# Output weights of a hybrid decoder layer: float16 halves and block sums prepared beside the attention and kept in DRAM, and all token tiles by block products

## The chip, the cores and the metric

The kernel runs on one core of a Trainium2 chip. The metric is the device time of one execution in microseconds (us), as the median of several runs. Beside it stands one profiled execution, from which every duration below is read. The engines are PE (TensorE, matrix products; PEld is its weight load), DVE (VectorE), ACT (ScalarE), POOL (GpSimd) and SP (SyncE, which here issues the DMAs). Each engine runs its own list of instructions in a fixed order.

## The reference

One layer over 2048 tokens (and 16 learned meta tokens ahead of them) of width 1024. Three mixers read one normalised input through one projection, and one output projection joins them:

```python
hn = rms_norm(h, pre_g)
proj = hn @ w_in                       # q, k, v, forget gate, GLA and RG-LRU columns
y_fox = fox_attention(q, k, v, log_f) * silu(fg)      # 8 heads of 64: width 512
y_gla = gla_chunked(...)  * silu(gg)                  # width 512
y_lru = rg_lru(...)       * silu(lg)                  # width 1024
y = concatenate([y_fox, y_gla, y_lru])                # 2048 wide
h = h + rms_norm(y @ w_out, post_g)                   # w_out is 2048 x 1024
```

`fox_attention` is causal softmax attention with a term c[t] - c[s] in the logit, c being the running sum of the log forget gates. Everything is float32; the kernel forms a float32 product from float16 halves, a value x scaled and split into hi + lo, and three products hi·hi, hi·lo and lo·hi.

## The kernel before, in words

The program is a list of jobs. Each job has a main part and a part that prepares the next job; `merge` (L155) takes them in turn, so that the matrix products of one fill the waits of the other. After that a scheduler puts the instructions of each engine in a fixed order. First come the projections and the mixing of GLA and of the LRU, up to about 890 us; then FoX, from 891 to 1706 us; then the output projection.

**FoX** goes over 4 pairs of heads p and 4 chunks c of 512 queries, 16 jobs, called (p,c) here. `fox_attend` (L1236 on) takes blocks of 128 keys one after another: 8 products into the one score pair `sq` (L1257), an Exp on ACT (`pt`, L1265), row sums on DVE and POOL (`za`, L1273), and 4 products with the values (`fv`, L1281). It ends with the row sums (`fx`, L1292), which go to DRAM and back in small steps (L499, L501, L506, L1299), a product on POOL (L1300) and the store of y (L1301).

Beside it `fox_prepare` of the next job projects keys, queries and values (L476, L488) and the gate, takes the maximum of every query block's scores (`mj` on DVE, L1207), and sends the maxima to the rows of `qx` by six small DMAs (`dr`, L1230). The first products of the next attend with `KX` wait for these. The gate (`fox_gate`) stands in the generator `rest`, whose pieces are handed out between the maxima. The weights of head pair p+1 are loaded by `load_dma` (L412) in jobs (p,1) and (p,3), and made into halves by ACT and DVE (L433, L434).

**The output projection** in its two forms. Tiles of 128 tokens 0 and 1 are done in 4 quarters of 256 columns and tiles 2 and 3 in 2 halves of 512 columns, by plain products over 16 k-tiles times 3 (`out_part`, L1566). The other 12 tiles are done as 6 pairs: y of a pair (256 x 2048) is cut into blocks A11, A12, A21, A22, and w_out into B11 to B22; with the sums S1 to S4 of the A and T1 to T4 of the B (T1 = B12 - B11, T2 = B22 - T1, T3 = B22 - B12, T4 = B21 - T2) seven block products of 24 matmuls give all four results (`out_pair`, L1586):

```python
def product(nm, w):            # 8 k-tiles, three float16 products each
    for kt in range(KT):
        for j, (a, b) in enumerate(((yh, wh), (yh, wl), (yl, wh))):
            nc.tensor.matmul(out=ps, lhsT=a[:, kt, :], rhs=b(kt), ...)
```

For this w_out is read from DRAM twice. `wout_begin` and `wout_end` take it in four column groups q (16 loads of 512 KB, a Square with a sum on ACT for the scale, then halves by ACT L1359 and DVE L1360); this begins in job (1,2) and goes on through (3,2), (3,3) and the first tiles. `sums_begin` and `sums_end` load it again (16 loads), form the T on POOL (L1386, L1390) and DVE (L1388, L1392) and split them into `ts`; they are placed among the plain tiles by a table in `project_out`. The y of a tile comes back from DRAM, is squared for its scale (L1418), and its maximum sum goes through one small product (`mx`, L463) before the halves are made.

The lines that the change and the prediction name are L412 to L415 (load of weights), L1188 (where `rest` holds the gate), L1230 to L1232 (dr), L1301 (store of y), and L1308 to L1480 with the table in `project_out`.

Of the kernel before, what the change touches and what calls it, by code (L numbers as in the profile page):

```python
# [21 lines left out]
P = 128  # L22
# [55 lines left out]
PLAIN = 4  # L78
OB = 27
# [8 lines left out]
class Ctx:  # L88
# [9 lines left out]
        "T": 3, "ZZ": 4, "WC": 1, "OO": 3, "OX": 2, "LV": 5, "AT": 2, "AC": 2, "GV": 6, "GG": 6, "GS": 6, "M": 1, "MV": 1, "YG": 2, "RS": 2, "ZS": 1, "ZA": 2, "PT": 6, "ED": 2, "KT": 1, "Z": 1, "WH": 1, "WL": 1, "XC": 4, "X": 16, "L0": 4, "L1": 4, "L2": 2, "L3": 2, "L4": 6}  # L98
# [68 lines left out]
def hybrid_kernel(tc, xT, x, w_grp, w_fa, vecs, w_a2, w_r, w_i, w_out, post_g, masks, out, yD=None):  # L167
    nc = tc.nc
    with ExitStack() as es:
# [13 lines left out]
        k.laD = k.dram.tile([P, T], F32, name="laD")  # L183
        k.xp = es.enter_context(tc.tile_pool(name="xhat", bufs=1))
# [4 lines left out]
        k.sent, k.begun, k.todo, k.wbegun, k.ybegun = [], [], [], [], []  # L189
# [19 lines left out]
        for t in range(8):  # L209
            for c in range(len(LP)):  # L210
# [20 lines left out]
        drain(jobs[0][1])
        for i, (_, _, mix, n_main, _) in enumerate(jobs):
# [8 lines left out]
            if i >= len(jobs) - 2:  # L241
# [326 lines left out]
def lru_mix(k, t, c, flush):  # L568
# [32 lines left out]
    for t, c, a, v, xc, h, gate in jobs:  # L601
# [9 lines left out]
        nc.sync.dma_start(out=k.yD[1024 + P * t:1024 + P * t + P, a0 - NM:u0 + n - NM], in_=y[:, a0 - u0:n])  # L611
# [555 lines left out]
def fox_prepare(k, p, c):  # L1167
# [20 lines left out]
    rest = chain(*([fox_values(k, p, 0)] if c == 0 else []), fox_values(k, p, c + 1), fox_gate(k, p, c))  # L1188
# [39 lines left out]
    for h in range(2):  # L1228
        for t in range(3):
            nc.sync.dma_start(out=qx[64 * h + t:64 * h + t + 1, :].rearrange("o (i q) -> o i q", q=P),  # L1230
                              in_=dr[4 * h:4 * h + 4, t, :])
    yield from rest  # L1232
    st["q", p, c] = qh, ql, qx


def fox_attend(k, p, c):  # L1236
# [64 lines left out]
    k.store = nc.sync.dma_start(out=k.yD[P * p:P * p + P, CH * c:CH * c + CH], in_=o).ins  # L1301

def out_begin(k):

    nc = k.nc  # L1308
    k.WH, k.WL = (k.xhl[:, i * OT * D:(i + 1) * OT * D].rearrange("p (k n) -> p k n", n=D) for i in range(2))
    k.winv = k.xhl[:, 2 * OT * D:2 * OT * D + 2 * CH].bitcast(F32)  # L1310
    k.wsc = {}
    yield from wout_begin(k, 0)
    yield from y_end(k)
    yield from wout_end(k)
    yield from wout_begin(k, 1)
    yield from y_begin(k, 1)
    yield from wout_end(k)
    yield from y_end(k)
    yield from wout_begin(k, 2)
    yield from y_begin(k, 2)  # L1320


def wout_load(k, q):

    raws = []
    for g in (q, q + 4):
        for h in range(2):
            raw = k.wp.tile([P, KT, P], F32, name="raw", bufs=RAWB)
            k.nc.sync.dma_start(out=raw, in_=k.ins["w_out"][g, h])
            raws.append(raw)  # L1330
    return raws
# [12 lines left out]


def wout_end(k):
    q, tiles, ss = k.wbegun.pop(0)
    sc, inv = scale_of(k, ss)
    k.wsc[q] = small(k, "wsc", [P, 1])
    k.nc.vector.tensor_copy(k.wsc[q], sc)  # L1350
    k.nc.gpsimd.tensor_scalar(out=k.winv[:, P * q:P * q + P], in0=k.ones, scalar1=inv, scalar2=None, op0=ALU.mult)
    for raw, hi, lo in tiles:
        halves(k, raw, sc, hi, lo)
# [51 lines left out]
def y_halves(k, plain=False):  # L1405
    if plain:
        hl = k.wk.tile([P, 2, KT, P], F16, name="yhl", tag="YP", bufs=6)
    else:
        hl = k.wp.tile([P, 2, KT, P], F16, name="whl", bufs=NWB)
# [3 lines left out]
def y_begin(k, t):  # L1413
    tiles = [(raw,) + y_halves(k, True) for raw in y_load(k, t)]
    ss = small(k, "ss", [P, 4], bufs=6)[:, 0:2]
    k.ybegun.append((t, tiles, ss))
    for i, (raw, _, lo) in enumerate(tiles):
        k.nc.scalar.activation(lo.bitcast(BF16), raw, AF.Square, accum_out=ss[:, i:i + 1])  # L1418
        yield


def y_end(k):
    if not k.ybegun:
        return
    t, tiles, ss = k.ybegun.pop(0)
    sc, inv = scale_of(k, ss)
    k.st["y", t] = [x[1:] for x in tiles], inv
    for raw, hi, lo in tiles:
        halves(k, raw, sc, hi, lo)
        yield  # L1430


def pair_halves(k, t):
# [3 lines left out]
    a11, a12 = y_load(k, t)  # L1437
    a21, a22 = y_load(k, t + 1)
# [30 lines left out]
def project_out(k):  # L1469

    nc = k.nc
    NT = SEQ // P
    k.TS, k.sbegun = [], []
# [4 lines left out]
    pairs = pair_halves(k, PLAIN)  # L1478
# [177 lines left out]
```

## Time and profile before

| | us |
|---|---|
| median of 3 runs (lowest to highest) | 2024.15 (2022.43 to 2024.53) |
| profiled execution | 2022.69 |
| its span, first to last instruction | 2020.9 |
| PE busy | 1898.0 (94%) |
| DVE / ACT / POOL busy | 1248.9 / 1004.8 / 591.0 |
| FoX | 891 to 1706 |
| output projection after FoX | 1706 to 2020.9 |

The profiled execution lies 1.5 us below the median, and 1.8 us of it lie around the span. The page shows the busy time of each engine, the span in 40 slices, and the groups of instructions; the trace behind it gives the timeline of each engine. In brackets at a row's end stands how long the engine was idle before that instruction, and what ended it. In the table of stretches the columns are the stretch, its length, and for each engine its busy time with the number of instructions, then the mean granted clock of PE as a share of 2.4 GHz, the DMA engines' busy share and the rate in GB/s. The jobs' bounds in it are the ends of the row-sum products (L1292).

### The profile page before, as it was taken

Reading aid. Unit: us, or ns where it says so; the run is one execution under the profiler, and the core shown is the slowest. Engines: PE = TensorE matmul, PEld = TensorE weight load, DVE = VectorE, ACT = ScalarE, POOL = GpSimd, SP = SyncE. Lnnn points to the kernel's source line nnn. Section 1 sums busy time; section 2 is a strip of 40 time slices with the busy share of each in tenths; the row PEclk is TensorE's granted clock in tenths of the full one; section 3 lists DMA queues with packets and bytes.
Section 4 is the critical chain, followed back from the end, with each engine's and each line's share of the span. In section 5 each row is a group of like instructions: output and inputs, shape, how many; then the busy total and the mean of one; then the engine's idle time right before and its main releaser. Section 6 shows DMA issues by size and latency. Waiting matters only on the chain. (4 is left out here: it accounts for less than half of the span.)

```text
span 2020.9 us, 39720 instructions
## 1 busy us (share of the span) xinstructions
PE 1898.0 (94%) x16240; PEld 1010.4 (50%) x16240; DVE 1248.9 (62%) x2786; ACT 1004.8 (50%) x1521; POOL 591.0 (29%) x566
## 2 busy tenths in 40 slices
PE   6888999999999999999999998999999869989998
PEld 5455666665555555554434433443344324534443
DVE  7665353454787787764674467346634755787664
ACT  7745643344888888842343234323432455545441
POOL 3434232332433333320122111211211112543532
PEclk9989999999999999999999999999999979999999
DMA  6200120211211111110030002000200132644321
GB/s 225 70 7 29 40 86 28 74 44 33 74 45 55 48 44 44 45 36 12 33 85 12 22 12 95 8 17 12 74 12 12 58 111 86 229 125 126 125 84 63
DMA packets 92263, 123.35 MB, mean 61 GB/s; under 512 B 16936, under 2 KB 59624, under 8 KB 92080
## 3 DMA queue, kind: packets, MB, share of 16 engines
q1 hardware_dynamic: 92080, 120.81, 18.6%
q8 instruction: 127, 2.08, 0.4%
q14 instruction: 56, 0.46, 0.1%
HBM read 94.03 MB, written 26.65 MB: 60 GB/s over the span
## 5 line engine op out<-in xcount | busy, mean ns | idle before, releaser
L476 PE MATMUL pj<-xhl,whl 128*128 128x512 f16 (+3 forms) x3960 | 800.1, 354 | 10.0 <-ACT whl L433 6.5
L476 PEld LDWEIGHTS <-whl 128*128 128x128 f16 x3984 | 364.4, 98 | 381.5 <-issue 52.8
L1265 ACT ACTIVATE pt<-sq,consts 128x1024 f32<-128x1024 f32 (+4 forms) x176 | 163.0, 926 | 282.1 <-PE sq L1263 151.8
L1207 DVE CUSTOM_DVE_ANT_0 mj<-mq,CB 128x512 bf16<-128x512 f32 (+4 forms) x344 | 189.7, 579 | 86.2 <-PE mq L1203 48.3
L1273 POOL TENSOR_TENSOR za<-za,pt 128x512 f32<-128x512 f32 (+1 forms) x80 | 97.8, 1223 | 404.6 <-ACT pt L1265 364.8
L488 PEld LDWEIGHTS <-xhl 128*128 128x128 f16 (+1 forms) x3264 | 192.7, 100 | 35.3 <-issue 30.7
L488 PE MATMUL pj<-whl,xhl 128*128 128x128 f16 (+1 forms) x3024 | 198.3, 224 | 0.0
L1273 DVE TENSOR_TENSOR za<-za,pt 128x512 f32<-128x512 f32 (+3 forms) x208 | 124.9, 627 | 118.1 <-ACT pt L1265 117.8
L1281 PE MATMUL fv<-pt,fv 128*64 128x512 f32 (+4 forms) x704 | 172.3, 537 | 0.4 <-ACT pt L1265 0.4
L1586 PEld LDWEIGHTS <-whl 128*128 128x128 f16 x1008 | 98.7, 98 | 126.1 <-issue 9.7
L1257 PE MATMUL sq<-QA,KA 64*128 64x512 f16 (+4 forms) x1032 | 129.9, 345 | 12.0 <-ACT pt L1265 11.6
L1586 PE MATMUL pj<-ts,whl 128*128 128x512 f16 x576 | 129.1, 383 | 6.3 <-ACT ts L1359 5.1
L554 DVE SCALAR_TENSOR_TENSOR xc<-lx,consts,xc 128x448 f32<-128x448 f32 (+1 forms) x120 | 94.0, 784 | 3.5
L1586 PE MATMUL pj<-xhl,whl 128*128 128x512 f16 x432 | 95.4, 379 | 0.0
L1566 PE MATMUL pj<-xhl,yhl 128*128 128x256 f16 (+1 forms) x576 | 90.1, 314 | 0.3 <-DVE xhl L1360 0.3
L1300 POOL TENSOR_TENSOR fo<-fo,rz 128x512 f32<-128x512 f32 x16 | 21.7, 1353 | 217.1 <-DMA rz<-rowD 196.0
L1257 PEld LDWEIGHTS <-KA 64*128 64x128 f16 (+1 forms) x1032 | 42.0, 94 | 79.5 <-issue 59.8
L1548 POOL TENSOR_TENSOR o<-o,xt 128x512 f32<-128x512 f32 x31 | 52.2, 1701 | 97.1 <-issue 65.9
L512 ACT ACTIVATE gate<-pj,consts 128x512 f32<-128x512 f32 (+2 forms) x72 | 46.1, 640 | 65.2 <-PE pj L476 64.1
L1257 PE MATMUL sq<-QA,KX 64*128 64x512 bf16 (+4 forms) x344 | 68.4, 342 | 9.8 <-DMA QA<-dr 9.8
L1566 PEld LDWEIGHTS <-yhl 128*128 128x128 f16 x576 | 56.0, 100 | 41.9 <-issue 13.1
L589 POOL TENSOR_TENSOR v<-a 128x448 f32<-128x448 f32 (+1 forms) x40 | 38.6, 965 | 128.2 <-ACT a L587 128.2
(263 smaller groups left out, 2847.5 us busy)
## 6 DMA issues: line engine op xcount, KB each, us to landing
raw<-in_w_grp_dram SPq DMA_DIRECT2D x44, 512.0 KB
raw<-in_w_out_dram SPq DMA_DIRECT2D x32, 512.0 KB
y<-yD SPq DMA_DIRECT2D x32, 512.0 KB
CB<-c32D SPq DMA_DIRECT2D x32, 256.0 KB
xt<-in_x_dram SPq DMA_DIRECT2D x16, 512.0 KB
out_dram<-o SPq DMA_DIRECT2D x32, 256.0 KB
yD<-yl SPq DMA_DIRECT2D x32, 224.0 KB
xr<-in_xT_dram SPq DMA_DIRECT2D x24, 256.0 KB
```

Of the source, the lines that this page charges most:

```text
L476: nc.tensor.matmul(out=ps, lhsT=a[:, kt, 0:m], rhs=b[:, kt, u0:u0 + n], start=i == 0, stop=i == 23)
L488: nc.tensor.matmul(out=ps, lhsT=a[:, kt, u0:u0 + m], rhs=b[:, kt, :], start=i == 0, stop=i == 23)
L512: k.act = nc.scalar.activation(out, ps, AF.Tanh, scale=hinv).ins
L554: nc.vector.scalar_tensor_tensor(out=xc, in0=lx[:, j:j + n], scalar=cw(j), in1=xc, op0=ALU.mult, op1=ALU.add)
L1207: nc.vector.tensor_tensor_reduce(out=junk[:, h, 0:n], in0=ps[:, h, 0:n], in1=d.cb[pc][:, h, 0:n], scale=1.0, scalar=-3e38, op0=ALU.add, op ...
L1257: nc.tensor.matmul(out=sp[0:m, h, off:], lhsT=a[j // 4][hs, kk], rhs=b[hs, off:], start=i == 0, stop=i == 3 and d < 0)
L1265: nc.scalar.activation(pt[0:m, :, off:], sp[0:m, :, off:], AF.Exp, scale=K.esc[0:m])
L1273: eng.tensor_tensor(out=za[h][0:m, off:], in0=za[h][0:m, off:], in1=pt[0:m, h, off:], op=ALU.add)
L1281: nc.tensor.matmul(out=pv[hs, off1:], lhsT=V1[0:m1, j1 % 4, hs], rhs=pt1[0:m1, h, off1:], start=j1 == 0, stop=j1 == nj - 1)
L1548: eng.tensor_tensor(out=o, in0=o, in1=xt[:, h, :], op=ALU.add)
L1566: nc.tensor.matmul(out=po, lhsT=a, rhs=cut(w, r), start=i == 0, stop=i == 3 * OT - 1)
L1586: nc.tensor.matmul(out=ps, lhsT=a[:, kt, :], rhs=b(kt), start=kt + j == 0, stop=(kt, j) == (KT - 1, 2))
```

## The change

`wout_ready` is a third generator that `merge` advances beside the FoX jobs. It loads w_out in 32 pieces of 256 KB, squares each on ACT (128x512), loads the 32 pieces again in 8 groups of four, forms T1 to T4 of each group by 4 subtractions on POOL, and splits the 7 blocks of each group into halves by ACT and DVE (56 of each, 128x512). Each pair of halves goes to `wD` in DRAM (56 stores of 256 KB). The loads are issued behind the last store of y or the last `dr` (`k.mark`, `issue_after`); so are now the loads of projection weights in `load_dma`.

`wout_load` brings the seven blocks back in 28 loads of 512 KB: 16 into the space of the normalised input, behind its last reader, and 12 into `ts`. All 8 pairs of tiles then go by block products (8 x 168 matmuls of 512 columns); the plain tiles, their table and `out_part` are gone. In `fox_prepare` the gate leaves `rest` and comes after the maxima and `dr`.

```diff
-def merge(main, fill, n_main, n_fill):
+def merge(main, fill, n_main, n_fill, side=iter(())):
     for i in range(n_main):
         next(main, None)
+        next(side, None)
...
-                if i == len(jobs) - 2:
-                    drain(y_begin(k, 0))
-            merge(mix, prep, n_main, n_fill)
+            if i == len(jobs) - 1:
+                drain(side)
+            merge(mix, prep, n_main, n_fill, side if i >= fox0 else iter(()))
...
 def load_dma(k, nm):
-    k.nc.sync.dma_start(out=raw, in_=src)
+    with k.tc.issue_after(k.mark) if k.mark is not None else nullcontext():
+        k.nc.sync.dma_start(out=raw, in_=src)
...
-    rest = chain(..., fox_values(k, p, c + 1), fox_gate(k, p, c))
+    rest = chain(..., fox_values(k, p, c + 1))
...
-            nc.sync.dma_start(out=qx[...], in_=dr[4 * h:4 * h + 4, t, :])
+            k.mark = nc.sync.dma_start(out=qx[...], in_=dr[4 * h:4 * h + 4, t, :]).ins
     yield from rest
+    yield from fox_gate(k, p, c)
...
+def wout_ready(k):
+    def load(q, b, j):
+        raw = k.wk.tile([P, KT // 2, P], F32, name="wr", tag="WR", bufs=BUFS["WR"])
+        with k.tc.issue_after(k.mark):
+            nc.sync.dma_start(out=raw, in_=k.ins["w_out"][...])
+        return raw
+    order = [(q, b, j) for q in range(4) for b in range(4) for j in range(2)]
+    for i, (q, b, j) in enumerate(order):
+        nc.scalar.activation(stage()[:, 0].bitcast(BF16), raws.pop(0), AF.Square, scale=2.0, accum_out=...)
+        if i + 3 < len(order):
+            raws.append(load(*order[i + 3]))
+        yield
+    for i, (q, j) in enumerate(groups):
+        (b11, b12, b22, b21), ahead = ahead, []
+        if i + 1 < len(groups):
+            ahead = [load(groups[i + 1][0], b, groups[i + 1][1]) for b in (0, 2, 3, 1)]
+        def minus(x, y):
+            t = k.wk.tile([P, KT // 2, P], F32, name="wt", tag="WT", bufs=BUFS["WT"])
+            nc.gpsimd.tensor_tensor(t, x, y, op=ALU.subtract)
+            return t
+        def put(nm, x):
+            hl = stage()
+            halves(k, x, k.wsc[q], hl[:, 0], hl[:, 1])
+            k.mark = nc.sync.dma_start(out=k.wD[BLOCKS.index(nm), :, j, :, q].rearrange(...), in_=hl).ins
+        t1 = minus(b12, b11)
+        put("B11", b11)
+        yield
+        t2 = minus(b22, t1)
+        put("T1", t1)
...
+def wout_load(k, nm, w):
+    with k.tc.issue_after(k.mark):
+        for z in range(2):
+            for j in range(2):
+                mark = k.nc.sync.dma_start(out=w[2 * z + j], in_=k.wD[BLOCKS.index(nm), z, j]).ins
...
-    for t in range(PLAIN, NT, 2):
-        more = pair_halves(k, t + 2) if t + 2 < NT else iter(())
-        out_pair(k, t, chain(pairs, more))
+    for t in range(0, NT, 2):
+        more = pair_halves(k, t + 2, pair_load(k, t + 2)) if t + 2 < NT else iter(())
+        out_pair(k, t, chain(k.pairs, more))
```

The order of the instructions on three places. In the changed kernel L1235 is `dr`, L1111 the load of `CB`, L419 the load of projection weights, L503, L505, L510 and L1306 the steps of the row sums, L1308 the store of y, L1326 the load of w_out, L1366 the store to `wD` and L1394 the load from it.

SP between jobs (1,2) and (1,3), in the kernel before: the two weight loads of head pair 2 (L415) stand between the two loads of `rz`, ahead of the store of y.

```order
L1230 DMA QA<-dr 1x4x128 x6
L506 DMA rowD<-consts 128x8
L1299 DMA rz<-rowD 64x512
L415 DMA raw<-in_w_grp_dram 128x1024 x2
L1329 DMA raw<-in_w_out_dram 128x1024
L1299 DMA rz<-rowD 64x512
L1301 DMA yD<-fo 128x512
```

The same place in the changed kernel:

```order
L1235 DMA QA<-dr 1x4x128 x6
L503 DMA rowD<-zs 1x512 x2
L505 DMA consts<-rowD 128x8
L510 DMA rowD<-consts 128x8
L1306 DMA rz<-rowD 64x512 x2
L1308 DMA yD<-fo 128x512
L419 DMA raw<-in_w_grp_dram 128x1024 x2
```

The weight loads (L419) moved behind the store of y, which waits for POOL's product.

ACT within job (1,0) of the changed kernel, where `pt` is the Exp of the attention, `KA` the keys of the next job, and L1424 a float16 half of a block (`wr`) or of a sum (`wt`):

```order
L1272 ACTIVATE pt<-sq,consts 128x1024
L1424 ACTIVATE ws<-wt,consts 128x512
L1424 ACTIVATE ws<-wr,consts 128x512
L1424 ACTIVATE ws<-wt,consts 128x512
L1085 ACTIVATE KA<-pj 128x512
L1424 ACTIVATE ws<-wt,consts 128x512
L1424 ACTIVATE ws<-wr,consts 128x512
L1424 ACTIVATE ws<-wt,consts 128x512
L1424 ACTIVATE ws<-wr,consts 128x512
L1272 ACTIVATE pt<-sq,consts 128x2x400
```

Seven halves now stand between one Exp and the next; three or four of them wait for a subtraction of POOL. The squares lie in the same way in jobs (0,0) to (0,3), and all 56 halves lie between the late part of (0,2) and the end of (1,1).

SP at the start of job (3,3) and through its end, in the changed kernel (`y` is the load of a pair of tiles, L1437):

```order
L1235 DMA QA<-dr 1x4x128 x6
L503 DMA rowD<-zs 1x512 x2
L505 DMA consts<-rowD 128x8
L510 DMA rowD<-consts 128x8
L1306 DMA rz<-rowD 64x512 x2
L1308 DMA yD<-fo 128x512
L1437 DMA y<-yD 128x8x128 x4
L1394 DMA xhl<-wD 128x2048 x6
L1394 DMA ts<-wD 128x2048 x2
L1394 DMA xhl<-wD 128x2048 x10
L1394 DMA ts<-wD 128x2048 x3
```

In the kernel before, the same place reads:

```order
L506 DMA rowD<-consts 128x8
L1230 DMA QA<-dr 1x4x128
L1299 DMA rz<-rowD 64x512 x2
L1230 DMA QA<-dr 1x4x128 x3
L1301 DMA yD<-fo 128x512
L1230 DMA QA<-dr 1x4x128 x2
L1401 DMA y<-yD 128x8x128 x4
L1329 DMA raw<-in_w_out_dram 128x1024 x4
```

The six `dr` of job (3,3) are one piece now, ahead of the row sums of (3,2); before, the store of y stood between them.

## Rows read from the trace of the kernel before

**Rows 1.** The page: PE's busy time in the span.

```profile
PE 1898.0 (94%) x16240; PEld 1010.4 (50%) x16240; DVE 1248.9 (62%) x2786; ACT 1004.8 (50%) x1521; POOL 591.0 (29%) x566
```

**Rows 2.** The chain that ended last, one piece: start us, us, what.

```profile
1850.18 36.28 PE pj L1586 x168
```

**Rows 3.** Stretches: (0,3) to (1,1), (1,2), (3,2), then up to (3,3), (3,3).

```profile
1037.40:1181.90 144.50, 142.15 (x1111) 65.10 (x1113) 73.83 (x219) 46.79 (x60) 27.02 (x22) 1.00 0.12 37
1181.90:1230.20 48.30, 46.06 (x325) 17.01 (x326) 35.97 (x103) 18.66 (x26) 9.07 (x9) 1.00 0.05 17
1575.50:1635.00 59.50, 51.33 (x334) 18.18 (x334) 43.27 (x120) 29.15 (x40) 11.92 (x11) 0.91 0.20 63
1635.00:1654.00 19.00, 7.36 (x59) 4.75 (x56) 9.53 (x26) 8.85 (x15) 1.26 (x1) 0.78 0.43 139
1654.00:1705.90 51.90, 46.34 (x286) 16.16 (x287) 28.36 (x49) 34.37 (x44) 14.08 (x10) 0.85 0.29 82
```

**Rows 4.** The plain tiles' products (L1566) alone in the last two stretches.

```profile
1635.00:1654.00 19.00, 5.04 (x43) 4.05 (x43) 0.78 0.43 139
1654.00:1705.90 51.90, 10.89 (x67) 5.79 (x68) 0.85 0.29 82
```

**Rows 5.** SP's timeline ahead of (3,3): start us, us, line, DMA.

```profile
1651.27 0.33 SPq L1301 DMA_DIRECT2D yD<-fo  x1
1651.64 1.20 SPq L1230 DMA_DIRECT2D QA<-dr  x2
```

**Rows 6.** PE's timeline ahead of (1,3): maxima turned, first products with KX.

```profile
1235.59 0.27 PE L1219 MATMUL fx<-consts 128*8 128x128 f32 x1
1243.77 0.39 PE L1257 MATMUL sq<-QA,KX 64*128 64x512 bf16 x1
```

**Rows 7.** PE's timeline after FoX, the three longest waits.

```profile
1733.98 0.19 PE L463 MATMUL mx<-consts 128*128 128x1 bf16 x2 [2.33 <-DVE consts L461]
1751.93 0.24 PE L463 MATMUL mx<-consts 128*128 128x1 bf16 x4 [1.79 <-DVE consts L461]
1793.59 0.59 PE L1586 MATMUL pj<-ts,whl 128*128 128x512 f16 x1 [5.13 <-ACT ts L1359]
```

**Rows 8.** Forms of lines L1359, L1530, L1360: duration in ns (lowest/median/highest).

```profile
L1359 ACT ACTIVATE ts<-t,consts x24: 704/708/722, 1718.8 to 1799.0; 128x512 f16<-128x512 f32 x24
L1530 ACT ACTIVATE sqo<-o x36: 398/629/631, 1645.3 to 2013.3; 128x512 bf16<-128x512 f32 x28, 128x256 bf16<-128x256 f32 x8
L1360 DVE SCALAR_TENSOR_TENSOR ts<-t,consts,ts x24: 734/748/2840, 1720.3 to 1800.7; 128x512 f16<-128x512 f32 x24
```

**Rows 9.** Groups of lines, 1705 to 1800: busy us, mean ns, idle before.

```profile
L1360 DVE SCALAR_TENSOR_TENSOR ts<-t,consts,ts 128x512 f16<-128x512 f32 x22 | 25.1, 1174 | 5.0 <-ACT ts L1359 4.8
L1386 POOL TENSOR_TENSOR t<-raw 128x1024 f32<-128x1024 f32 x4 | 11.3, 2833 | 28.4 <-DMA raw<-in_w_out_dram 12.3 <-DVE consts L1540 8.2 <-DMA rowD<-consts 4.4
```

**Rows 10.** Timelines of DVE and POOL at one place among the plain tiles.

```profile
1763.47 4.94 DVE L1360 SCALAR_TENSOR_TENSOR ts<-t,consts,ts 128x512 f16<-128x512 f32 x2 [3.00 <-ACT ts L1359]
...
1765.07 2.79 POOL L1390 TENSOR_TENSOR raw<-raw 128x1024 f32<-128x1024 f32 x1
```

**Rows 11.** SP's store of y after (1,1), a weight load of (1,2), its square.

```profile
1199.06 0.32 SPq L1301 DMA_DIRECT2D yD<-fo  x1
...
1243.73 1.59 SPq L415 DMA_DIRECT2D raw<-in_w_grp_dram  x2
...
1248.05 1.06 ACT L450 ACTIVATE whl<-raw 128x1024 bf16<-128x1024 f32 x1 [2.58 <-DMA raw<-in_w_grp_dram]
```

**Rows 12.** ACT's timeline: squares of w_out, each waiting for its 512 KB load.

```profile
1639.32 1.06 ACT L1342 ACTIVATE junk<-raw 128x1024 bf16<-128x1024 f32 x1 [0.62 <-DMA raw<-in_w_out_dram]
1641.68 1.06 ACT L1342 ACTIVATE junk<-raw 128x1024 bf16<-128x1024 f32 x1 [1.21 <-DMA raw<-in_w_out_dram]
```

**Rows 13.** After FoX: SP's load of a y tile and ACT's square of it.

```profile
1723.27 0.42 SPq L1401 DMA_DIRECT2D y<-yD  x1
...
1729.63 1.04 ACT L1418 ACTIVATE yhl<-y 128x1024 bf16<-128x1024 f32 x1
```

More of the change, by code (lines that the diff above doesn't have):

```diff
@@ L1313, in out_begin @@
[L1313 to L1331, printed above, removed]
@@ L1346, in wout_end @@
[L1346 to L1353, printed above, removed]
+    k.W = {}
+    n = 4 * KT // 2 * P
+    views = [[k.xhl[:, (4 * i + z) * n:(4 * i + z + 1) * n].rearrange("p (q k n) -> p q k n", q=4, n=P)
+              for z in range(4)] for i in range(4)]
@@ L1354, in wout_end @@
+    k.winv = k.xhl[:, 16 * n:16 * n + 2 * CH].bitcast(F32)
+    wout_load(k, BLOCKS[0], views[0])
+    raws = pair_load(k, 0)
+    for i in range(1, 4):
+        k.load = wout_load(k, BLOCKS[i], views[i])
+    for q in range(4):
+        nc.gpsimd.tensor_scalar(out=k.winv[:, P * q:P * q + P], in0=k.ones, scalar1=k.winvs[q], scalar2=None,
+                                op0=ALU.mult)
+    yield
+    yield
+    k.pairs = pair_halves(k, 0, raws)
+    for _ in range(5):
+        next(k.pairs)
         yield
@@ L1402, in y_load, with y_halves, pair_load, pair_halves @@
     return raws
[L1405 to L1409, printed above, removed]
-    return hl[:, 0], hl[:, 1]
[L1413 to L1433, printed above, removed]
+def y_halves(k):
+    hl = k.wp.tile([P, 2, KT, P], F16, name="whl", bufs=NWB)
+    return hl[:, 0], hl[:, 1]
+def pair_load(k, t):
+    return y_load(k, t) + y_load(k, t + 1)
+def pair_halves(k, t, raws):
     nc = k.nc
-    a11, a12 = y_load(k, t)
-    a21, a22 = y_load(k, t + 1)
+    a11, a12, a21, a22 = raws
     junk = k.wk.tile([P, KT, P], BF16, name="junk", tag="A2", bufs=BUFS["A2"])
@@ L1472, in project_out @@
     NT = SEQ // P
-    k.TS, k.sbegun = [], []
+    k.mark = k.load
+    for nm in BLOCKS[4:]:
+        wout_load(k, nm, [k.wk.tile([P, 4, KT // 2, P], F16, name="ts", tag="TS", bufs=BUFS["TS"])
+                           for _ in range(4)])
     pg = unit(k, "WC", [P, 2, CH], name="pg")
@@ L1509, in __init__ @@
         self.o = unit(k, "OO", [P, 2, CH], name="o")
-    def take(self, x, inv, half, cols):
-        k, nc = self.k, self.k.nc
-        m, n = (1, half) if half is not None else (2, slice(0, 2))
-        o, w = self.o[:, n, cols], k.winv[:, cols]
-        if half is None:
-            w = w.unsqueeze(1).to_broadcast([P, 2, cols.stop - cols.start])
-        nc.vector.scalar_tensor_tensor(out=o, in0=x, scalar=inv, in1=w, op0=ALU.mult, op1=ALU.mult)
-        self.square(o)
     def scaled(self, half):
@@ L1575, in out_pair @@
     inv = d["inv"]
-    block = lambda r, h: tuple((lambda kt, w=w: w[:, KT * r + kt, CH * h:CH * h + CH]) for w in (k.WH, k.WL))
-    sums = lambda i: tuple((lambda kt, z=z: k.TS[i][z][kt // 4][:, kt % 4, :]) for z in range(2))
-    full = slice(0, CH)
     def product(nm, w):
@@ L1603, in out_pair @@
     ob.scaled(1)
-    add(product("A22", sums(3)), c21, c21)
+    add(product("A22", "T4"), c21, c21)
     ob.scaled(0)
     ob.finish()
-    add(product("S4", block(1, 1)), c12, c12)
+    add(product("S4", "B22"), c12, c12)
     oa.scaled(1)
```

152 lines of the change are left out of this document (62 added, 90 removed).

## The prediction

> **What bounds the kernel now.** I read the page first. PE is busy for 94% of the span [rows 1], so time goes either where PE has columns to multiply or where it waits. The chain of waits comes next: it ends in the pairs' block products, 36.28 us a pair [rows 2], with no wait between, and each matmul of 512 columns takes 36.28/168 = 0.216 us. The table of stretches then says where PE is not busy. In a clean FoX job such as (1,2) it is busy for 46.06 of 48.3 us, DVE for 35.97, and POOL has 9.07. Three stretches near the end differ: (3,2) takes 59.5 us, the time up to the first scores of (3,3) 19.0, and (3,3) 51.9 with a granted clock of 0.85 [rows 3]. There w_out's squares and halves run beside FoX. The timeline of PE after FoX adds three waits [rows 7]. So the bound is PE, and the change can give back PE's columns and these waits; it can lose where it puts new work beside FoX.
>
> **Columns.** The plain tiles 0 to 3 have 2 x 4 x 48 matmuls of 256 columns and 2 x 2 x 48 of 512: 196,608 columns. Two pairs by blocks have 2 x 168 x 512 = 172,032. The 24,576 fewer cost 0.216/512 us each: -10.4 us. The products of 256 columns are taken at the same rate per column.
>
> **After FoX.** The three waits of 2.33, 1.79 and 5.13 us [rows 7] lie in code that goes: -9.3. One is new. Pair 0's y is loaded behind the store of (3,2), but the y of pair 1 stands in SP's order behind the store of (3,3), some 17 us after FoX's end: (1,1) ended at 1181.9 and its store came at 1199.06 [rows 3, 11]. Before, the load of y at 1723.27 was followed by its square at 1729.63, 6.4 us later [rows 13]. Pair 1 has four tiles; at one load per 2.4 us [rows 12] the fourth is squared at 17 + 6.4 + 3 x 2.4 = 31 us, and scale and halves add some 3. PE reaches pair 1's scale product after about 136 of pair 0's 168 matmuls, 29 us past the end of FoX. The wait is 5 us by this; loads of the weights in the same queue add some, and I take 8 (0 to 18). Sum of the part: -1.3.
>
> **(3,2), and the way into (3,3).** w_out's squares and halves leave (3,2), which then looks like (1,2): 59.5 to 48.3, less 0.5 us of plain products in it that are counted above: -10.7. In the 19.0 us up to (3,3)'s scores, 43 of the plain matmuls of 256 columns are included, 43 x 0.107 = 4.6 us [rows 4]. The rest, 14.4, is waiting for `dr`: SP had the last two behind the store of y at 1651.27 [rows 5], which itself waited for POOL. In the new order all six stand together ahead of the row sums. The clean case, ahead of (1,3), takes from 1235.59 to 1243.77, or 8.2 us [rows 6]. With no filler there PE waits through it: -5.9 us (0 to -10, if the gate, now behind `dr`, covers part of it). In (3,3) ACT keeps 4 squares and 7 halves of y, 13 us instead of 19; 67 plain matmuls (7.1 us) leave and 18 of the first block product (3.9 us) come in. I take 47 us for 51.9, which is -1.7 without the columns.
>
> So far: -10.4 - 1.3 - 10.7 - 5.9 - 1.7 = -30.
>
> **The work beside FoX.** It lies in the 144.5 us from (0,3)'s start to (1,1)'s end, the squares a job or three earlier. ACT: 32 squares at 0.63 + 0.19 and 56 halves at 0.71 [rows 8], 26 + 40 us. DVE: 56 halves between 0.75 [rows 8] and 1.17, the mean beside POOL's subtractions [rows 9], 42 to 66 us. POOL: 32 subtractions at half of 2.83 [rows 9], 45 us. With the present 73.8, 46.8 and 27.0 [rows 3] this makes 116 to 140 us of DVE, at most 113 of ACT and 72 of POOL in 144.5: each fits, DVE barely. Fitting is not enough, since the engines keep an order: up to seven halves lie between one Exp and the next, some behind a POOL subtraction, and the store to `wD` waits for DVE with the next `dr` behind it on SP. PE has few waits there now, 2.4 us in all, and fillers. Bounds: (3,2) has 10.5 us more of ACT and 7.3 more of DVE than (1,2) and takes 11.2 us longer [rows 3]; at that ratio of 0.63 the 120 us added on the two engines would cost 75. At the other end, where PE's fillers cover all, it is -1. In (3,2) 5.3 of the 11.2 us are PE's own busy time, at a granted clock of 0.91, after it had waited, and fillers were short there; in (0,3) to (1,1) PE is busy for 98% and at full clock, with projections to fill. That is the nearer case, and I take +8.
>
> That POOL can hold up DVE the trace shows: a half of 0.748 us took up to 2.84, where POOL's L1390 ran from 1765.07 to 1767.86 [rows 8, 10]. Yet the mean of 22 halves beside subtractions is 1.17, not 0.75 + 2.8 [rows 9], so most go through unhindered or wait for a part. The Trainium skill, "SBUF — State Buffer", section "SBUF: two separate sides", has a rule that speaks against the change: a VectorE operation with two SBUF inputs and a GpSimd operation that reads SBUF share a port as an exclusive lock, and whichever comes second is blocked for the whole instruction of the first. The trace agrees in the single case of rows 10; by the rule the sum would be that of rival B, by the mean of rows 9 the +8 above.
>
> **Weights of the next head pair.** In `load_dma` the loads now wait for the last store. For (p,2) to (p,3) they come behind the store of y, about 17 us after the end of (p,2), instead of 13.5 (1243.73 against 1230.2) [rows 3, 11]. The load lands 4.3 us later (1248.05), and the squares and scale follow, so at 23 us; PE has 26 projection matmuls and four or five unfilled attend steps of 2.4 us before it wants the scale, and is there at about 18. Three head pairs at 5 to 6 us, of which some 3 each were waited already: +8 (0 to +25, if the halves behind ACT's Exps take 4 us more at each place and nothing else fills).
>
> **Elsewhere.** Loads of LRU weights stand behind the store of y and land a little later; there are fillers and a pass of slack: 0 (0 to +4). The tail after the last product stays.
>
> **Sum.** -30 + 8 + 8 = -14 against the profiled execution's 2022.7, which is 1.5 below the median of 2024.15: 2008.7, and I forecast 2009.
>
> **Rivals.**
> A. The new work is hidden. For it: PE waits only a few us in these jobs, the projections fill, and ACT and POOL are at a third and a fifth of their time. Against it: the order on ACT and SP. The side work costs nothing and the weights 0 to 2: 2022.7 - 30 + 1 = about 1993.
> B. FoX slows down (the other side). Place: (0,3) to (1,1). Halves on DVE wait for POOL's subtractions as in rows 10, POOL's own products with `rz` and `za` wait behind subtractions, and the `za` of a block holds the buffer of the next Exp; `dr` on SP waits behind stores to `wD`. Price: if DVE and POOL never ran at once, as in rows 10, their 116 + 72 = 188 us would stand in 144.5, up to +43 (maxima read from PSUM, so a part of it is likelier: +30), and the weights come to +15. From +35 of both together, 2022.7 - 30 + 35, the time is above 2028; likely value 2038.
> C. The start of the output part is held by loads. 28 loads of 512 KB and the y of two pairs have to land, 32 x 2.4 = 77 us at the rate of rows 12, from 14 us after (3,2)'s end on, so until about 91; FoX ends some 56 after it. T1 is the fifth product, needed 17 us after FoX's end, the last ones at 27; loads 24 and 28 of 28 land at 20 and 29 us past it. Waits of 3 to 10 us beyond the 8 already taken: 2017. Against it: the loads in these rows waited for buffers too, so the rate may be higher.
> The change does what it says in any case: the columns are in the program's list.
>
> **Chances.** Forecast 0.42, A 0.24, B 0.22, C 0.12. Shorter than 2020 means faster by over 0.2%, about what a measurement of this kernel can tell from no change; 2020 to 2028 is the same. The forecast's own range is 2000 to 2018. Faster: 0.41 + 0.24 + 0.06 = 0.71; same: 0.01 + 0.05 of C + 0.03 of B = 0.09 or a little more, 0.10; slower 0.19. The range for 8 in 10 reaches from A's low end, 1986, to 2034, in the middle of B.
>
> **What would show it.** Columns: pairs of 36.28 us, eight of them. (3,2) at 48 us and the way into (3,3) at about 8 show the clean end. In (p,3) a PE wait at `mx` or at the first projection with the new weights, of 5 us or more, shows the late loads; none there refutes that term. In (0,3) to (1,1) a stretch of 144.5 + 8 is the forecast, +0 is A, +25 or more is B; then POOL and DVE waits show whether it was their lock. A PE wait at the first of pair 1 of about 8 us confirms the y chain, waits at T1 or T4 are C. Wrong is the forecast above all if FoX's stretches before (3,2) grow by more than 30 us in all.

## The result, and the profile after

The changed kernel takes 2070.74 us (median of 4 runs, 2066.12 to 2073.45) against 2024.34 for the kernel before: ratio 1.0227, 95% interval 1.0205 to 1.0249. The forecast was 2009, with a range from 1986 to 2034. The sign was wrong, and the time lies above the range.

The page of the changed kernel gives the span and the busy time:

```profile
span 2070.5 us, 39449 instructions
PE 1918.2 (93%) x15988; PEld 990.9 (48%) x15988; DVE 1284.5 (62%) x2802; ACT 1011.7 (49%) x1561; POOL 641.6 (31%) x596
```

PE has 252 matmuls fewer than in [rows 1] and is busy for 20 us longer. A pair of tiles still takes 36.28 us, as in [rows 2], so the extra time is not in the output products.

The bounds of the FoX jobs, read from the row-sum products (L1292, now L1299), show where it is. Lengths in us, before and after, (0,0) counted from the span's start:

| job | before | after | | job | before | after |
|---|---|---|---|---|---|---|
| up to (0,0)'s end | 941.5 | 962.7 | | (2,0) | 32.6 | 35.6 |
| (0,1) | 43.8 | 53.4 | | (2,1) | 43.8 | 51.8 |
| (0,2) | 52.2 | 52.0 | | (2,2) | 48.3 | 46.5 |
| (0,3) | 68.2 | 89.1 | | (2,3) | 70.6 | 69.7 |
| (1,0) | 32.6 | 47.5 | | (3,0) | 32.6 | 35.6 |
| (1,1) | 43.8 | 52.3 | | (3,1) | 43.7 | 46.1 |
| (1,2) | 48.3 | 47.2 | | (3,2) | 59.4 | 46.2 |
| (1,3) | 73.8 | 70.3 | | (3,3), with the way in | 70.9 | 57.6 |
| | | | | after FoX | 315.0 | 306.7 |

The end gained 35 us against the 30 of the sum: 13.2 in (3,2), 13.3 up to the end of (3,3), 8.3 after FoX. Everything ahead of it lost 84. Three places carry it: 21 us before the first FoX job ends, 10 in (0,1), 44 in (0,3) to (1,1).

The stretches of the changed kernel that answer to [rows 3], in its order of columns, are (0,3) to (1,1), then (3,2), then (3,3) with the way into it:

```profile
1068.10:1257.00 188.90, 161.48 (x1159) 71.75 (x1157) 141.83 (x294) 88.13 (x135) 83.36 (x55) 0.92 0.49 153
1660.00:1706.20 46.20, 43.05 (x276) 15.04 (x275) 33.05 (x94) 15.52 (x19) 10.67 (x9) 1.00 0.04 13
1706.20:1763.80 57.60, 44.31 (x235) 12.48 (x236) 35.49 (x40) 29.15 (x34) 21.84 (x13) 0.82 0.63 225
```

DVE went from 73.83 to 141.83 us in the first of them and POOL from 27.02 to 83.36; PE is idle for 27 us of it instead of 2.4, and busy for 19 us longer (161.48 against 142.15, with 48 more matmuls) at a granted clock of 0.92 instead of 1.00.

The chain that ended last in the changed kernel, from the end of FoX on (start, length, what), has the new wait that the prediction named:

```profile
1768.23 5.04 DMA consts<-rowD
...
1776.44 4.98 DMA rz<-rowD
1781.58 1.27 POOL fo L1307
1782.87 0.33 SPq L1308
...
1785.38 9.17 DMA y<-yD
1794.72 2.32 POOL s L1468
1797.07 1.23 DVE s L1469
1798.29 2.23 DVE consts L465
1800.57 0.27 PE mx L467 x4
1800.84 25.89 PE pj L1553 x110
```

PE's timeline at that point puts the wait at 7.34 us, forecast 8:

```profile
1800.57 0.27 PE L467 MATMUL mx<-consts 128*128 128x1 bf16 x4 [7.34 <-DVE consts L465]
```

### The profile page after: what moved, and what is told of

Read it like the earlier page. It is cut to its first block, busy times and chain, and to the rows that moved or that the text cites. A ratio compares the mean times of both kernels' runs of the same rounds, so it can differ in the third digit from the quotient of the medians.

```text
span 2070.5 us, 39449 instructions
## 1 busy us (share of the span) xinstructions
PE 1918.2 (93%) x15988; PEld 990.9 (48%) x15988; DVE 1284.5 (62%) x2802; ACT 1011.7 (49%) x1561; POOL 641.6 (31%) x596
## 2 busy tenths in 40 slices
DMA packets 116135, 152.70 MB, mean 74 GB/s; under 512 B 18792, under 2 KB 75816, under 8 KB 115952
## 5 line engine op out<-in xcount | busy, mean ns | idle before, releaser
L480 PE MATMUL pj<-xhl,whl 128*128 128x512 f16 (+3 forms) x3960 | 809.6, 356 | 9.1 <-ACT whl L437 4.2
L480 PEld LDWEIGHTS <-whl 128*128 128x128 f16 x3984 | 364.9, 98 | 391.2 <-issue 68.7
L1553 PEld LDWEIGHTS <-whl 128*128 128x128 f16 x1344 | 131.0, 98 | 164.4 <-issue 8.1
L1280 DVE TENSOR_TENSOR za<-za,pt 128x512 f32<-128x512 f32 (+3 forms) x208 | 135.5, 675 | 92.0 <-ACT pt L1272 91.1
L1288 PE MATMUL fv<-pt,fv 128*64 128x512 f32 (+4 forms) x704 | 187.4, 549 | 2.1 <-ACT pt L1272 1.9
L1553 PE MATMUL pj<-xhl,whl 128*128 128x512 f16 x768 | 169.1, 380 | 0.0
L558 DVE SCALAR_TENSOR_TENSOR xc<-lx,consts,xc 128x448 f32<-128x448 f32 (+1 forms) x120 | 98.9, 824 | 3.4
L1204 PE MATMUL mq<-KA,QA 64*128 64x512 f16 (+4 forms) x344 | 61.4, 345 | 21.8 <-DVE consts L1212 20.8
L1519 ACT ACTIVATE sqo<-o 128x512 bf16<-128x512 f32 x32 | 20.1, 629 | 123.4 <-DVE o L1513 123.4
L1559 DVE SCALAR_TENSOR_TENSOR o<-pj,consts,o 128x512 f32<-128x512 f32 x56 | 41.1, 745 | 59.1 <-PE pj L1553 54.8
L517 DVE SCALAR_TENSOR_TENSOR gate<-gate,pj 128x512 f32<-128x512 f32 (+2 forms) x72 | 45.2, 628 | 43.2 <-ACT gate L516 41.7
```

The costliest lines, as they stand in the source:

```text
L480: nc.tensor.matmul(out=ps, lhsT=a[:, kt, 0:m], rhs=b[:, kt, u0:u0 + n], start=i == 0, stop=i == 23)
L558: nc.vector.scalar_tensor_tensor(out=xc, in0=lx[:, j:j + n], scalar=cw(j), in1=xc, op0=ALU.mult, op1=ALU.add)
L1204: nc.tensor.matmul(out=ps[:, h, 0:n], lhsT=qh[hs, P * i:P * i + P], rhs=d.hi[pc][hs, 0:n], start=True, stop=pc < c)
L1280: eng.tensor_tensor(out=za[h][0:m, off:], in0=za[h][0:m, off:], in1=pt[0:m, h, off:], op=ALU.add)
L1288: nc.tensor.matmul(out=pv[hs, off1:], lhsT=V1[0:m1, j1 % 4, hs], rhs=pt1[0:m1, h, off1:], start=j1 == 0, stop=j1 == nj - 1)
L1553: nc.tensor.matmul(out=ps, lhsT=a[:, kt, :], rhs=w[b + kt // 4][:, :, kt % 4, :], start=kt + j == 0, stop=(kt, j) == (KT - 1, 2))
```

## The experiments

Times are medians; each ratio is to runs of the kernel before on the same chip. "The three jobs" are (0,3), (1,0) and (1,1): 144.5 us before, 188.9 in the changed kernel.

**Weight loads of the LRU stage at once (e1a).** The edit takes the mark from the LRU's store of y, so that `load_dma` has nothing to wait behind until FoX:

```diff
-        k.mark = nc.sync.dma_start(out=k.yD[1024 + P * t:...], in_=y[...]).ins
+        nc.sync.dma_start(out=k.yD[1024 + P * t:...], in_=y[...])
```

> The changed kernel, with the weight loads of the LRU stage issued at once again instead of behind the last store of y. The first FoX job of the changed kernel ends 21 us later than before (962.7 against 941.5), and ACT waited 11.0 us in 9 waits for weights there, before none. Late-load theory: the waits of ACT's squares for the loads go, the first job of FoX ends 12 to 20 us earlier, time about 2053 to 2058. Rival (the work beside FoX and the other placement of buffers slow the stage): under 4 us, 2067 to 2072.

Measured 2051.81 us, ratio 1.0126 (1.0102 to 1.0150), 19 us below the changed kernel. The first FoX job ends at 950.4 instead of 962.7; the rest comes back in later jobs, none over 3 us. ACT's waits from 500 us on up to there (engine, line, what ended the wait: us in total, times, longest), in the changed kernel:

```profile
ACT xcs L560 <- DVE xc L558: 45.8, 28, 2.0
ACT whl L454 <- DMA raw<-in_w_grp_dram: 11.0, 9, 3.4
```

and with the loads at once, where the second row has no counterpart:

```profile
ACT xcs L560 <- DVE xc L558: 35.9, 29, 2.5
```

The square of a weight stands at a fixed place in ACT's list. When its load comes late, ACT stands still there, and the LRU's own steps behind it come late: the waits for `xcs` fall back to about the 34.7 us of the kernel before.

**FoX's weight loads behind `dr` (e1c).** As the last, with a mark of its own for `load_dma` that only the `dr` transfers set.

> As e1a_lru_at_once, and the weight loads of FoX's next head pair are issued behind the six dr transfers instead of behind the store of y, some 10 us earlier. Late-load theory: ACT's waits for weights in FoX (24 us over the 6 loaded jobs in the changed kernel) shrink, 8 to 15 us below e1a, about 2042 to 2048. Rival (PE fills these waits with other work): within 3 us of e1a.

2032.95 us, ratio 1.0048 (1.0026 to 1.0071): 19 us below the last one, more than expected. The gain lies in the jobs that prepare with these weights: (0,3) 81.2, (1,3) 65.1, (2,1) 47.8, (2,3) 66.9, against 88.8, 70.5, 51.8 and 70.7 in e1a. ACT's waits for weights in FoX, in the changed kernel:

```profile
ACT whl L454 <- DMA raw<-in_w_grp_dram: 23.9, 8, 4.4
```

and in e1c:

```profile
ACT whl L454 <- DMA raw<-in_w_grp_dram: 2.2, 2, 1.3
```

Late loads thus cost 38 us in all. In FoX the wait begins on ACT and is passed on to PE. In (0,3) of the changed kernel ACT's square waits for the load, DVE's next step for the square, and PE's scale product (`mx`) for DVE:

```profile
1090.53 1.06 ACT L454 ACTIVATE whl<-raw 128x1024 bf16<-128x1024 f32 x1 [4.39 <-DMA raw<-in_w_grp_dram]
...
1091.71 0.16 DVE L465 CAST consts<-consts 128x1 bf16<-128x1 f32 x1 [3.65 <-ACT whl L454]
...
1091.92 0.16 PE L467 MATMUL mx<-consts 128*128 128x1 bf16 x1 [4.91 <-DVE consts L465]
```

At the scale products of the weights in (0,3), (1,3) and (2,3) PE waited for 10.0 us in e1a (4.65, 2.75 and 0.20, 2.36) and for 1.3 in e1c. The four jobs together became 20.8 us shorter: 12.0 of it is idle time of PE, and 8.8 is busy time of PE, whose granted clock went from 0.90 to 0.94 in (0,3) and from 0.97 and 0.98 to 1.00 in (2,1) and (2,3).

**The gate back among the maxima (e2)**, in the changed kernel.

```diff
-    rest = chain(..., fox_values(k, p, c + 1))
+    rest = chain(..., fox_values(k, p, c + 1), fox_gate(k, p, c))
...
-    yield from fox_gate(k, p, c)
```

> The changed kernel with the gate back among the maxima, ahead of dr. Gate theory: the four jobs of head pair 2 took 203.7 us in the changed kernel and 195.3 before without any side work in them, because the gate's matmuls moved from jobs that waited for filler, (2,2) and (2,3), to (2,0) and (2,1), which had none to spare; with the gate back these jobs take 195 to 197 again, and about 8 us come back in each of three head pairs, less some 5 at the way into (3,3): time 2050 to 2060. Rival (the lengthening of (2,1) comes from the late weights, and the gate behind dr is a gain): 2070 to 2078.

2050.02 us, ratio 1.0126 (1.0109 to 1.0142). The time is as the gate theory said, and head pair 2 takes 198.2 us, near its 195 to 197. But ACT's waits for weights fell from 23.9 to 5.2 us in FoX, so the edit also took away part of the late-load cost by another order on ACT. The next two runs show that gate and loads do not simply add up:

**The gate's move alone, in the kernel before (e6).**

> The kernel before with the gate's move alone: maxima and dr first, the gate behind them. Gate theory: the filler moves from (p,2) and (p,3) to (p,0) and (p,1), which have none to spare; 5 to 8 us lost in each of three head pairs, some 8 gained on the way into (3,3): 2032 to 2042. Rival (the move is worth the wait for dr and costs nothing): 2010 to 2020.

2024.51 us, ratio 1.0013 (0.9999 to 1.0027): no difference, and in neither range. Two effects cancel. Every (p,0) and (p,1) is 2 to 5 us longer, as the gate theory said; (p,3) is 1 to 6 us shorter, and (0,2) and (3,2) are 5 and 6 us shorter. Up to the end of (3,1) the move costs 11.2 us, and (3,2) and (3,3) give 11.7 back. The net loss I expected of it is refuted.

**Gate back in all jobs but (3,3), loads behind `dr` (f1).**

> e1c_behind_dr with the gate back among the maxima in every job but the last, (3,3), where it stays behind dr. If the parts add up: 2033 less 21 (what e2_gate_back gave on the changed kernel) less 8 (the way into (3,3) took 65.0 us there with the gate ahead, 57 with it behind): 2003 to 2012, faster than the kernel before. Rival (the gains overlap, since late weights and missing filler hit the same waits of the attention): 2016 to 2025.

2038.61 us, ratio 1.0077 (1.0054 to 1.0100), in neither range, and not faster than with the gate behind `dr` everywhere. The two gains do not add up. (0,1) gained 9 us, but (0,3) took 93.2 and (1,3) 77.2.

**Without the subtractions (e4)**, in the changed kernel: `minus` returns its first operand.

> The changed kernel with the 32 subtractions on POOL left out: the halves of the sums are taken from raw blocks, so the sums are wrong. All squares, halves, stores and loads stay. POOL theory (DVE is held up by POOL's subtractions and ACT's halves wait for them ahead of an Exp): the three jobs (0,3), (1,0), (1,1) took 188.9 us against 144.5 before; they fall to 150 to 165, time 2045 to 2055. Rival (DVE's and ACT's halves by themselves, or the transfers): they stay above 178, time 2060 to 2070.

2053.13 us, ratio 1.0137 (1.0120 to 1.0154); the three jobs take 173.3. The time is in the range of the POOL theory, the three jobs in neither. So 15.6 us hang on POOL's work, and 28.8 are left.

**Spreading the work on w_out (f2, f4).** Both start from f1; the first advances it on two of three steps, the second on all steps but those of (p,2).

```diff
-        next(side, None)
+        if i % 3:
+            next(side, None)
```

> f1_gate_last with the work on w_out advanced on two of three steps of the attention only, so that its 56 halves lie 14 each in (1,2), (1,3), (2,1) and (2,3) instead of 52 in (0,3) and (1,0). Density theory (the engines' in-order waits cost where halves stand closely): the side work costs half or less of its 30 us, 1988 to 1998. Rival (each half and subtraction costs the same wherever it stands): as f1 within 4 us.

> f1_gate_last with the work on w_out advanced on every step but those of the jobs (p,2), where DVE is busy for 36 of 48 us; its halves lie 14 in (1,1), 20 in (1,3), 19 in (2,0) and 3 in (2,1). Density theory: between f1 and f2, 1992 to 2002, with most of the loss in (2,0), where 19 halves stand in 33 us. Rival (DVE's idle share in a job decides): at or below f2.

2055.44 (1.0164, 1.0142 to 1.0185) and 2041.55 us (1.0093, 1.0070 to 1.0117), against 2038.61. The density theory is wrong. In f2, with 14 or 15 halves each, (1,2) took 61.7 us, (1,3) 91.3, (2,1) 52.3 and (2,3) 84.4: the loss goes where the work goes, and here it became larger. f4 cannot be told from f1 within the noise; that it lies below f2 is what its rival, DVE's idle share, had said. In both runs no half lies in (0,3), only 9 and 15 squares, and it still takes 79.2 and 79.4 us against 68.2 before. So the squares cost time too.

**Loads of w_out's second pass free of the stores to `wD` (h1)** (the store no longer sets the mark).

> e1c_behind_dr with the loads of w_out's second pass no longer issued behind the last store to wD, only behind the last store of y or dr. In e1c ACT waited 20 us for such loads ahead of its squares and halves, and POOL 7. Load theory: these waits go and some 10 us come back in (0,3) and (1,0), about 2022 to 2026. Rival (what is waited for on ACT are POOL's sums and DVE, or the loads' buffers): within 4 us of 2033.

2055.72 us, ratio 1.0157 (1.0135 to 1.0179): slower, neither of the two expected. The order changed with it: 14 halves each moved into (1,2) and (1,3), which took 59.1 and 76.0 us. This run agrees with f2 and says nothing clear about the loads.

**ACT against DVE (h2, h4, h3).** Three kernels on the base of e1c. In h2, DVE makes the high halves; in h4, the squares too; in h3, subtractions and low halves are left out.

```diff
-            halves(k, x, k.wsc[q], hl[:, 0], hl[:, 1])
+            nc.vector.tensor_scalar(out=hl[:, 0], in0=x, scalar1=k.wsc[q], scalar2=None, op0=ALU.mult)
+            nc.vector.scalar_tensor_tensor(out=hl[:, 1], in0=x, scalar=k.wsc[q], in1=hl[:, 0], ...)
```

> e1c_behind_dr with the high halves of the w_out blocks made by DVE instead of ACT: 56 fewer operations of 0.71 us on ACT, 56 more on DVE. ACT-order theory (a half that waits for its input on ACT holds the Exp behind it, and the attention has one score buffer): (0,3) to (1,1) fall from 178.7 to 160 or less, about 2013 to 2020. DVE theory (DVE is the engine that is full there, and maxima and row sums come late): they grow, 2038 to 2050.

> h2_halves_dve with the 32 squares of w_out on DVE too, so that ACT has none of the new work beside FoX. ACT-order theory: (0,0) to (0,2) fall by another 8 to 12 us, about 2003 to 2012. DVE theory: longer still than h2, 2045 to 2060.

> e1c_behind_dr without the 32 subtractions and without DVE's 56 low halves: the high halves of raw blocks are stored twice, so the output weights are wrong. ACT's squares and halves, the loads and the stores stay. DVE and POOL theory: (0,3) to (1,1) fall to 150 or less, 2000 to 2006. ACT theory: the halves still stand ahead of the Exps, though their inputs are only loads: 158 to 168, 2012 to 2020.

2047.71 (1.0123, 1.0098 to 1.0147), 2047.40 (1.0114, 1.0089 to 1.0139) and 2008.36 us (0.9922, 0.9902 to 0.9943). h2 and h4 lie in the ranges of the DVE theory, h3 between its two. Relieving ACT at DVE's expense lost 15 us; relieving DVE and POOL gained 25. The table of stretches over the three jobs, in the order of columns of [rows 3], gives for e1c:

```profile
1055.30:1234.00 178.70, 156.63 (x1159) 71.72 (x1157) 141.98 (x294) 88.74 (x135) 80.86 (x55) 0.96 0.51 161
```

For h2, with DVE's high halves:

```profile
1050.30:1252.10 201.80, 162.48 (x1187) 72.30 (x1186) 172.59 (x354) 54.01 (x80) 78.55 (x55) 0.92 0.45 143
```

For h3, without low halves and subtractions:

```profile
1051.40:1204.40 153.00, 147.15 (x1149) 66.89 (x1149) 75.76 (x237) 86.68 (x134) 28.41 (x23) 1.00 0.58 188
```

ACT has 87 us of work and the DMA engines are busy for 0.58 of the time in h3, and the clock stays at 1.00. What DVE does, and what POOL does beside it, sets most of the length. PE pays for it twice: between h3 and e1c its idle time grows by 16.2 us (from 5.9 to 22.1), and its busy time by 9.5 for 10 matmuls more, at a granted clock of 0.96.

**The square completed (i1, i4, i2)**: subtractions alone, low halves alone, and all of it with the subtractions on DVE.

> e1c_behind_dr without DVE's 56 low halves (the high halves are stored twice, so the output weights are wrong); POOL's 32 subtractions stay. Amount theory (DVE's added 57 us are the loss): (0,3) to (1,1) near h3's 153, 155 to 160, time 2010 to 2016. Hold-up theory (POOL's subtractions stop DVE's own FoX work): 165 to 172, 2020 to 2027.

> e1c_behind_dr without POOL's 32 subtractions (the sums are taken from raw blocks, so they are wrong); DVE's 56 low halves stay. Amount theory: 170 to 176 us for (0,3) to (1,1), time 2025 to 2031. Hold-up theory: 158 to 165, 2013 to 2020, and DVE's low halves at 0.75 to 0.80 us instead of 1.05.

> e1c_behind_dr with the 32 subtractions on DVE instead of POOL: DVE has some 20 us more work, POOL none of the new. Hold-up theory: DVE's low halves and row sums fall back to their lone durations, which saves about what the subtractions cost it: (0,3) to (1,1) 170 to 180, 2025 to 2035, though POOL's 56 us are gone. Amount theory: 190 to 200, 2043 to 2055.

2017.36 (0.9940, 0.9920 to 0.9959), 2016.10 (0.9941, 0.9925 to 0.9958) and 2026.90 us (1.0001, 0.9989 to 1.0012). The three jobs in the same table, first with the subtractions alone (i1):

```profile
1054.00:1217.90 163.90, 150.58 (x1151) 69.01 (x1150) 84.05 (x237) 87.55 (x134) 70.89 (x55) 0.98 0.56 176
```

With the low halves alone (i4):

```profile
1058.40:1219.50 161.10, 151.69 (x1157) 68.48 (x1157) 118.06 (x294) 87.13 (x135) 29.48 (x23) 0.99 0.57 179
```

With all of it, the subtractions on DVE (i2):

```profile
1055.00:1227.90 172.90, 156.84 (x1190) 70.65 (x1188) 138.53 (x330) 88.17 (x136) 30.57 (x23) 0.97 0.54 167
```

Over h3's 153.0 the subtractions cost 10.9 us, the low halves 8.1, both together 25.7: 6.7 more than the sum. i4 and i2 lie in the ranges of the hold-up theory, i1 between the two; amount and hold-up both count. The hold-up is in the durations (busy us, mean ns, idle before). With the subtractions on POOL (e1c):

```profile
L1424 DVE SCALAR_TENSOR_TENSOR ws<-wt,consts,ws 128x512 f16<-128x512 f32 x32 | 34.0, 1070 | 3.8 <-ACT ws L1423 3.7
L1279 DVE TENSOR_TENSOR za<-za,pt 128x512 f32<-128x512 f32 x20 | 21.1, 1079 | 3.4 <-ACT pt L1271 3.4
...
L1359 POOL TENSOR_TENSOR wt<-wr 128x512 f32<-128x512 f32 x16 | 25.7, 1606 | 27.0 <-DVE consts L1211 11.7 <-PE sq L1263 5.6 <-DMA wD<-ws 4.9
```

With the subtractions on DVE (i2):

```profile
L1424 DVE SCALAR_TENSOR_TENSOR ws<-wt,consts,ws 128x512 f16<-128x512 f32 x32 | 25.1, 798 | 1.8 <-ACT ws L1423 1.6
L1279 DVE TENSOR_TENSOR za<-za,pt 128x512 f32<-128x512 f32 x20 | 16.4, 844 | 2.2 <-ACT pt L1271 2.2
L1359 DVE TENSOR_TENSOR wt<-wr 128x512 f32<-128x512 f32 x16 | 10.9, 682 | 2.7 <-DMA yD<-fo 2.6
```

A low half falls from 1.07 to 0.80 us, a row sum from 1.08 to 0.84, and a subtraction takes 0.68 on DVE instead of 1.61 on POOL. The other corners of the square agree: a row sum takes 0.76 us in h3, 0.81 with the low halves alone, but 1.00 with the subtractions alone. DVE's busy time in the three jobs is smaller with the subtractions (138.53) than without them (141.98), and 6 us come back. The Trainium skill, "SBUF — State Buffer", section "Who interferes with whom", says that a VectorE instruction with two SBUF inputs contends with a GpSimd instruction that reads SBUF; a low half and a row sum have two such inputs, the subtraction reads SBUF, and these means agree.

**What is left, and a faster version.** The gate among the maxima for (0,0) to (0,2) alone, on i2; then also the second head's row sums on POOL in the three jobs.

> i2_sums_dve with the gate back among the maxima for the jobs (0,0) to (0,2) alone. Gate theory: (0,1) falls from 54.8 to 46 or 47, the later jobs stay, 2016 to 2021, a little faster than the kernel before. Rival ((0,1) waits for w_out's squares or its transfers): 2025 to 2029.

> j1_gate_early with all row sums of the second head on POOL in the jobs (0,3), (1,0) and (1,1): some 14 additions of 0.9 us less on DVE, of 1.3 us more on POOL. Load theory: (0,3) to (1,1) fall by 5 to 10 us from 173, 2008 to 2014. Hold-up theory (POOL's additions stop DVE for as long as they save it): within 3 us of j1.

2016.82 us, ratio 0.9978 (0.9968 to 0.9988), and 2018.80 (0.9988, 0.9976 to 0.9999). In j1 (0,1) falls from 54.8 to 46.8 as expected, while (0,2) rises from 50.0 to 57.1, because the edit puts 369 matmuls of PE there instead of 296; with (0,0) earlier the gain is 6 us at (0,2)'s end. j1 beats both kernels, the one before by 0.2% only. In j2 the three jobs take 172.5 against 174.2: the load theory is refuted here. With 13 instructions fewer DVE is busy for only 1.1 us less (137.99 against 139.13), since its low halves of the sums grow from 0.79 to 0.92 us beside POOL's additions.

## Why the prediction was wrong

**The end of the program came out right in the sum, with errors that cancel.** It gained 35 us for the 30 forecast. (3,2) measured 46.2 for 48.3 and the wait for pair 1 7.34 for 8. But the way into (3,3) took 4.2 us (1706.2 to 1710.4) for 8.2, and (3,3) itself 53.4 for 47: PE waited for 4.13 us at pair 0's scale product and for 3.77 at an Exp in it, at a granted clock of 0.82. That these two add up to about the forecast is luck. Three small slips stand beside them: 14.4 less 8.2 is 6.2 and not 5.9; [rows 6] leave out PE's first product with `KX`, which stood at 1240.57, 5.0 us behind the maxima and not 8.2; and -14 from the profiled 2022.7 makes a median of 2010. Nor did the sum have a term for what the gate's move costs ahead of (3,2), 11.2 us in the kernel before (e6).

**"Elsewhere ... 0 (0 to +4)" failed first.** I wrote that the LRU's weight loads land a little later and that fillers and slack cover it. There is no slack on ACT's list: it stood for 11.0 us at squares waiting for weights, and with the loads at once 19 us came back.

**"Weights of the next head pair: +8" had the right place and less than half the size.** I followed the weights to PE's scale product in (p,3), and there PE did wait: 10.0 us in e1a, 1.3 in e1c, near the 8. The price was 19. Two things are missing from the term. It counted one of the two jobs in which a head pair's weights arrive; the other is (p,1), and there (2,1) lost 4.0 us ((0,1) and (1,1) hold work on w_out as well). And it took the wait alone: 8.8 us of the 20.8 in the four jobs are PE's busy time. The first to wait was ACT's square, as in the kernel before [rows 11]; its waits for weights were 23.9 us and fell to 2.2. That the Exps behind the square added to the price is not shown: the waits of PE's score products for an Exp did not fall (6.4 us in e1a, 11.4 in e1c, from 962 to 1700 us).

**"The work beside FoX: +8" was a term of 30.** The three jobs grew by 44.4 us in the changed kernel, 34.2 with the late loads gone. 4.1 of these stand in e6 as well, 148.6 us with 1151 matmuls for 1111 and no new work: that is the gate. Of the other 30, DVE's low halves and POOL's subtractions make 25.7 (h3 against e1c); the 4.4 left, ACT's squares and halves, loads and stores among them, were not taken apart. That is rival B's place and its price of +30, and in part its mechanism: moving the subtractions from POOL to DVE gives 5.8 us in these jobs.

My argument that it fits into 144.5 us was one from busy shares: DVE was to be busy for 116 to 140 of 144.5, and I called that covered. But DVE's maxima are a link between PE's products, and its row sums feed the end of each job. When its list is full, PE waits at the next maxima, as PE's row in the waits of the changed kernel from 1000 to 1200 us shows (us in total, times, longest):

```profile
PE mq L1204 <- DVE consts L1212: 12.0, 5, 4.6
```

[rows 3] have no wait of that kind worth 3 us in the whole stretch, since PE idled for 2.4 us there. In e1c a step of DVE ended 15.4 of PE's 22.1 us of waits in the three jobs, one of ACT 6.7. The ratio from (3,2), 0.63 us lost per us added, was set aside because fillers were at hand; it would have given 75 us. Measured are 30 for the 120 us that I had added, 0.25 for one, where I had taken 0.07. The true price lay between the row and the argument from idle time, and neither had it.

**Ahead of (3,2)** the 84 us are then, by the ends of the jobs: late loads 35 (the changed kernel against e1c at (3,1)'s end), the gate 11 (e6), the work in the three jobs 30, and some 8 in (0,1), which takes 55.9 us in e1c and 47.8 with the gate's move alone (e6). There PE waits for w_out's own scale product, which I had not priced; in e1c:

```profile
971.68 0.16 DVE L1343 TENSOR_REDUCE consts<-consts 128x1 f32<-128x8 f32 x1 [4.30 <-ACT ws L1337]
...
972.09 0.16 PE L467 MATMUL mx<-consts 128*128 128x1 bf16 x1 [2.33 <-DVE consts L465]
```

DVE's sum waits for ACT's squares of w_out (L1337), and PE for the sum. PE is idle for 4.6 us of (0,1) and its granted clock is 0.91; in e6 these are 0.1 us and 1.00. With the gate among the maxima (j1) no such wait is left in (0,1). Why (0,3) is shorter with the gate behind `dr` (81.2 in e1c, 93.2 in f1) stays open.

## What to carry to other kernels

A load that is moved behind another transfer is paid for by the first instruction that reads it on an in-order engine, by everything behind that instruction there, and by what waits for its result on other engines; list every place where such a load stands, and price the chain and not the consumer's wait alone. Work added beside a latency-bound stage is not free because an engine has idle time: ask which of its results the stage waits for within a step. A stretch that already has such work gives one bound and the idle time the other; here they lay at 75 and 8 us around a measured 30. Where DVE and POOL both read two operands from SBUF, try the subtraction on DVE: here DVE's own busy time fell by it.

## What the runs showed of the hardware that was not expected

A 128x512 float32 subtraction took 1.53 to 1.94 us on POOL beside DVE's low halves, 1.32 without them (i1), and 0.68 to 0.78 on DVE. DVE's total busy time fell when it took over all 32 of them, from 141.98 to 138.53 us in the three jobs. And the DMA engines moved 188 GB/s in the three jobs of h3, against 153 in the changed kernel, with the attention at full clock beside it: the 29 MB of extra transfers over the whole span (152.70 against 123.35) can have cost these jobs no more than the 4.4 us that were not taken apart.
